# Two transformer blocks on one core: another order of the seven products of a weight block, and other places for its weight quarters

## The chip, the cores and the metric

The kernel runs on one core of a Trainium2 chip. The metric is the device time of one execution in microseconds (us). Before the change it is 1966.29 us, the median of three runs (1965.46 to 1967.71).

## The reference, cut to what matters

The reference computes two transformer blocks on a sequence of 512 tokens with 1024 channels, in float32. Each ends with a gated feed-forward part; the hidden width is 2816. The change touches only its first half, in both blocks:

```
h = rmsnorm(x, g)                      # [512, 1024]
a, u = h @ Wa, h @ Wu                  # each [1024, 2816]
hidden = silu(a) * u                   # [512, 2816]
x = x + hidden @ Wdown                 # not touched
```

In the first block Wa and Wu are the two halves of `w_ffn_in`, in the second they are `w_ffn_gate_2` and `w_ffn_up_2`.

## The kernel before, in words

TensorE (PE) gets float32 precision from three products of rounded halves: every operand is split into a high half (`wh`, a cast on ACT) and a low half (`wl`, a subtraction on VectorE, DVE), and one product is high x high + high x low + low x high (lines 1029 to 1031). Splitting a 128x1024 weight tile is therefore one cast on ACT (L170) and one subtraction on DVE (L171).

The hidden columns come in eleven slices of 256 columns of Wa and the same of Wu. The first two slices (`N_PLAIN`) are plain products (`gemm_quarters`, lines 275 to 277). Each of the other nine is a `Block`: a product of 2 x 2 quarters by Strassen's scheme in Winograd's form, seven products in place of eight. The rows of the weights are cut in two halves and the columns in two, which here are the slice of Wa and that of Wu. A product is 24 matmuls of 128x256 (2 column tiles, 4 steps of k, 3 halves), so a stage of nine blocks has 63 products or 1512 matmuls. Nine blocks in each of the two feed-forward parts: call them stage 1 and stage 2, and count blocks from 0.

The seven weight operands of a block are T1 to T7. T1, T2 and T3 are plain quarters of the weights. T5 and T7 are sums of two quarters that the DMA makes: SP loads one quarter into a tile, and then GpSimd's queue (POOL) issues a second transfer that adds the other quarter into it (`accum_op`, L994). T6 = T1 + T7 overwrites T1 (DVE, L1005), and T4 = T2 + T6 overwrites T2 (DVE, L1008). All activations' operands S1 to S7 are ready before the first block.

`woven` sets the order of the products: in a block 1, 2, then 3 of the block before, 6, 7, then 4 of the block before, 5. `play` goes through that list and splits two products ahead: while product n runs, `prep` of product n+2 is issued. `prep` takes a place for `wh` and one for `wl`, of which there are three each, so the cast of a product can start when the product three places earlier has been read. `prep` then makes the sums of T6 and T4, and last it issues a load of the block after: `prep` of 6 loads its T1, of 7 its T7, of 5 its T5, of 3 its T3, and of 1 its T2.

The places of the tiles: `raw` has three, which T1 (later T6), T5 and T7 share with all plain weight loads; T2 and T3 take places of `S`, of which there are 18, 16 of them with the activations' halves. A load waits until its place is free. The SP and POOL queues, like the engines, work in the order in which their instructions stand; a scheduler lays them out, near the order of the source. When a product is done, `after` copies or adds the sums in PSUM (ACT L1038, DVE L1040, L1043, L1048), and `out` makes the gated product (ACT L1129, DVE L1130, L1135). PSUM bank A holds the sums of products 1, 6, 5, 3, bank B product 2, bank C products 7 and 4.

Of the kernel before, what the change touches and what calls it, by code (L numbers as in the profile page):

```python
# [9 lines left out]
F32 = mybir.dt.float32  # L10
# [57 lines left out]
SLOTS = {"p": 32, "t": 12, "k": 3, "raw": 3, "wh": 3, "wl": 3}  # L68

MIX = {"q": 36}  # L70
FFN = {"S": 18}

STEP = 0.65
SB_FILL = (1.14, 1.5, 0.46)
# [5 lines left out]
N_PLAIN = 2  # L80
# [40 lines left out]
def run(gen):  # L121
    for _ in gen:
        pass


def build(tc, A, dump=None):
    nc = tc.nc
    with ExitStack() as es:
# [25 lines left out]
        def wtile(tag, shape, dt):  # L154
            if tag in SLOTS:
                return P.tile(shape, dt, tag=tag, name=tag, bufs=SLOTS[tag])
            return region["pool"].tile(shape, dt, tag=tag, name=tag, bufs=region["slots"][tag])
# [29 lines left out]
        def weights(w, k0, kn, c0, ncol):  # L187
            if low_engine["e"] is None:

                raw = wtile("raw", [128, kn, ncol], F32)  # L190
                nc.sync.dma_start(raw, w[k0 * 128:(k0 + kn) * 128, c0:c0 + ncol].rearrange("(k p) n -> p k n", p=128))
                wh = wtile("wh", [128, kn, ncol], F32R)
                wl = wtile("wl", [128, kn, ncol], F32R)
                nc.scalar.copy(wh, raw)
                nc.scalar.activation(wl, f(wh), AF.Copy, scale=-1.0)
                nc.gpsimd.dma_start(wl, raw, accum_op=ALU.add)
                return wh, wl
            raw = wtile("raw", [128, kn, ncol], F32)
            nc.sync.dma_start(raw, w[k0 * 128:(k0 + kn) * 128, c0:c0 + ncol].rearrange("(k p) n -> p k n", p=128))
            wh = wtile("wh", [128, kn, ncol], F32R)  # L200
            wl = wtile("wl", [128, kn, ncol], F32R)
            nc.scalar.copy(wh, raw)  # L202
            low_engine["e"].tensor_tensor(out=wl, in0=raw, in1=f(wh), op=ALU.subtract)  # L203
            return wh, wl
# [58 lines left out]
        def gemm_quarters(w, c0, X, evac, n0=0):  # L263

            ws = [weights(w, b, 4, c0, 256) for b in (0, 4)]
            for hf in range(2):
                ps = psum("gz"[hf])
                for n in range(2):
                    s = slice(n * 128, n * 128 + 128)
                    for k in range(KD):  # L270
                        wh, wl = ws[k // 4]
                        xh, xl = X.at(k, hf)
                        o = ps[:, n * 256:n * 256 + 256]
                        st, sp = n == 0 and k == 0, n == 1 and k == KD - 1
                        nc.tensor.matmul(o, wh[:, k % 4, s], xh, start=st, stop=False, skip_group_check=True)
                        nc.tensor.matmul(o, wh[:, k % 4, s], xl, start=False, stop=False, skip_group_check=True)
                        nc.tensor.matmul(o, wl[:, k % 4, s], xh, start=False, stop=sp, skip_group_check=True)
                for n in range(2):
                    evac(n0 + n, hf, ps[:, n * 256:n * 256 + 256])
# [62 lines left out]
        cols = small("cols", NVEC)  # L342
# [156 lines left out]
        for k in range(KD):  # L499
# [7 lines left out]
            for n, off in enumerate((0, 128, 512, 640, 256, 384)):  # L507
                s = slice(off, off + 128)
# [228 lines left out]
        for h in range(4):  # L737
# [20 lines left out]
            for c in range(2):  # L758
                run(gemm(w_in, KD, 7168 + 512 * h + 256 * c, H, ev_g, n0=2 * c))
                if c == 0:  # L760
                    ada_next()
                    for j in range(4):
# [6 lines left out]
                        s = new("t")  # L769
# [6 lines left out]
            for e in range(4):  # L776
# [10 lines left out]
                s = new("t")  # L787
# [46 lines left out]
        show("merged", [merged[n] for n in range(8)])  # L834
        lay_out(FFN)

# [76 lines left out]
        class Normed:  # L913
# [3 lines left out]
            def __init__(self):  # L917
                self.X = [new("p") for _ in range(KD)]
                self.Q = {}
                self.S = {}  # L920
# [51 lines left out]
        class Block:  # L972

            def __init__(self, rows, cols, X, out):
                self.rows, self.cols, self.X, self.out = rows, cols, X, out
                self.kn = len(rows[0])
                self.T, self.w, self.ps, self.sb = {}, {}, {}, {}
                self.done = set()  # L980
# [5 lines left out]

            def load(self, n):

                (i, j), more, tag = {1: ((1, 1), None, "raw"), 2: ((2, 1), None, "S"), 3: ((2, 2), None, "S"),
                                     5: ((1, 2), (1, 1), "raw"), 7: ((1, 2), (2, 2), "raw")}[n]  # L990
                t = self.T[n] = wtile(tag, [128, self.kn, 256], F32)
                nc.sync.dma_start(t, self.part(i, j))
                if more:
                    nc.gpsimd.dma_start(t, self.part(*more), accum_op=ALU.add)  # L994

            def prep(self, i):

                T = self.T
                wh = wtile("wh", [128, self.kn, 256], F32R)
                wl = wtile("wl", [128, self.kn, 256], F32R)  # L1000
                split(T[i], wh, wl)
                self.w[i] = wh, wl
                if i == 1:
                    T[6] = T.pop(1)
                    nc.vector.tensor_add(T[6], T[6], T[7])  # L1005
                if i == 2:
                    T[4] = T.pop(2)
                    nc.vector.tensor_add(T[4], T[4], T[6])  # L1008
                if i == 6:
                    del T[6]  # L1010

            BANK = {1: "A", 6: "A", 5: "A", 3: "A", 2: "B", 7: "C", 4: "C"}
# [38 lines left out]
        def play(blocks):  # L1051

            steps = woven(blocks)
            after = dict(zip(blocks, blocks[1:]))
            for i in (1, 7, 2, 5, 3):
                blocks[0].load(i)

            def prep(b, i):
                b.prep(i)
                load = {6: 1, 7: 7, 5: 5, 3: 3, 1: 2}.get(i)  # L1060
                if b in after and load:
                    after[b].load(load)
            for b, i in steps[:2]:
                prep(b, i)
            for n, (b, i) in enumerate(steps):
                if n + 2 < len(steps):
                    prep(*steps[n + 2])
                b.product(i)

        def woven(blocks):  # L1070

            steps = []
            for n, b in enumerate(blocks + [None]):
                a = blocks[n - 1] if n else None
                steps += [(c, i) for c, i in ((b, 1), (b, 2), (a, 3), (b, 6), (b, 7), (a, 4), (b, 5)) if c is not None]
            return steps

        class Split:
# [21 lines left out]
        def ffn_hidden(wa, ca, wu, cu, X):  # L1100

            hid = [new("p") for _ in range(2 * N_PLAIN)]
            sums = X.sums()
            act = {}

            def ev_a(n, hf, ps):
                s = new("t")[:, 0:256]
                if n not in act:
                    act[n] = new("t")
                nc.scalar.activation(s, ps, AF.Sigmoid)  # L1110
                nc.vector.tensor_mul(act[n][:, HS[hf]], ps, s)

            def ev_u(n, hf, ps):
                nc.vector.tensor_mul(hid[n][:, HS[hf]], ps, act[n][:, HS[hf]])
            for c in range(N_PLAIN):
                gemm_quarters(wa, ca + 256 * c, X, ev_a, n0=2 * c)
                gemm_quarters(wu, cu + 256 * c, X, ev_u, n0=2 * c)
                for _ in range(4):
                    next(sums, None)
            run(sums)  # L1120
            blocks = []
            for s in range(N_PLAIN, 11):
                hold = {}
                hid += [new("p") for _ in range(2)]

                def out(i, j, c, s=s, hold=hold):
                    if j == 1:
                        g = new("t")
                        nc.scalar.activation(g, c, AF.Sigmoid)  # L1129
                        nc.vector.tensor_mul(c, c, g)  # L1130
                    hold[i, j] = c
                    if (i, 1) in hold and (i, 2) in hold:
                        for e in range(2):
                            es = slice(e * 256, e * 256 + 256)
                            nc.vector.scalar_tensor_tensor(out=hid[2 * s + e][:, HS[i - 1]], in0=hold[i, 2][:, es], scalar=-1.0,  # L1135
                                                           in1=hold[i, 1][:, es], op0=ALU.mult, op1=ALU.mult)
                blocks.append(Block((range(0, 4), range(4, 8)), ((wa, ca + 256 * s), (wu, cu + 256 * s)), X, out))
            play(blocks)
            lay_out(MIX)
            return Split(hid, ["q" if 2 <= i < 20 else "p" for i in range(KF)])  # L1140
# [32 lines left out]
        w2 = A["w_in_2"]  # L1173
# [13 lines left out]
        for k0 in (0, 4):  # L1187
            raw = wtile("raw", [128, 4, 56], F32)
# [343 lines left out]
        for h in range(0, 8, 2):  # L1532
            t = new("k" if h < 4 else "q").rearrange("p (h c) -> p h c", h=2)
# [45 lines left out]
        bg.drain()  # L1579
        lay_out(FFN)  # L1580
        show("cat", [cat[n] for n in range(8)])
# [22 lines left out]
        for b in range(2):  # L1604
# [23 lines left out]
            for t in range(4):  # L1628
                for h in held:
                    products(t, *h)  # L1630
                s = new("t")
# [46 lines left out]
```

## Time and profile before

| | |
|---|---|
| median of three runs | 1966.29 us |
| the profiled execution | 1966.17 us |
| its span | 1964.5 us |
| stage 1, first matmul to last | 916.5 to 1124.5 us of the span |
| stage 2, first matmul to last | 1625.4 to 1832.7 us |
| TensorE busy over the span | 94% |
| DVE, ACT, POOL busy | 62%, 43%, 17% |

The span runs from the first to the last instruction on the core; the execution's own time is 1.7 us longer. TensorE's time counts as busy while any matmul is in its pipe, and a matmul stays there longer (0.28 us) than the distance to the next (0.12 us), so a short wait shows as less idle time than it costs.

### The profile page before, as it was taken

Reading aid. Unit: us, or ns where it says so; the run is one execution under the profiler, and the core shown is the slowest. Engines: PE = TensorE matmul, PEld = TensorE weight load, DVE = VectorE, ACT = ScalarE, POOL = GpSimd, SP = SyncE. Lnnn points to the kernel's source line nnn. Section 1 sums busy time; section 2 is a strip of 40 time slices with the busy share of each in tenths; the row PEclk is TensorE's granted clock in tenths of the full one; section 3 lists DMA queues with packets and bytes.
Section 4 is the critical chain, followed back from the end, with each engine's and each line's share of the span. In section 5 each row is a group of like instructions: output and inputs, shape, how many; then the busy total and the mean of one; then the engine's idle time right before and its main releaser. Section 6 shows DMA issues by size and latency. Waiting matters only on the chain. (4 is left out here: it accounts for less than half of the span.)

```text
span 1964.5 us, 28367 instructions
## 1 busy us (share of the span) xinstructions
PE 1847.1 (94%) x11145; PEld 1622.2 (83%) x11145; DVE 1211.6 (62%) x1980; ACT 844.9 (43%) x1400; POOL 334.1 (17%) x397
## 2 busy tenths in 40 slices
PE   6889999999999999999888899979999899889998
PEld 4678887888888898889888888858887799889887
DVE  7888875645465654656666642467577575666622
ACT  3556653233323223344444442474365544444522
POOL 3232221112020302011111002122234201111000
PEclk8999999999999999999999999979999999999999
DMA  7512222533334244426766523266453137666222
GB/s 230 187 54 67 64 74 92 164 113 110 124 107 135 78 148 151 160 65 164 158 150 151 134 93 116 71 161 152 96 143 104 44 97 155 156 155 168 95 88 75
DMA packets 224929, 238.29 MB, mean 121 GB/s; under 512 B 10902, under 2 KB 207524, under 8 KB 224796
## 3 DMA queue, kind: packets, MB, share of 16 engines
q1 hardware_dynamic: 199424, 197.91, 32.6%
q0 software_dynamic: 25024, 38.44, 10.7%
q8 instruction: 87, 1.43, 0.3%
q14 instruction: 46, 0.38, 0.1%
q10 hardware_dynamic: 348, 0.13, 0.0%
HBM read 217.56 MB, written 9.99 MB: 116 GB/s over the span
## 5 line engine op out<-in xcount | busy, mean ns | idle before, releaser
L203 DVE TENSOR_TENSOR wl<-raw,wh 128x1024 fp32r<-128x1024 f32 x190 | 236.8, 1246 | 223.7 <-ACT wh L202 222.2
L202 ACT CAST wh<-raw 128x1024 fp32r<-128x1024 f32 x190 | 197.9, 1041 | 387.2 <-PE ps_g L181 190.1
L180 PE MATMUL ps_g<-p,wh 128*128 128x512 f32 (+1 forms) x824 | 327.6, 402 | 8.4 <-DVE q L1184 3.7
L181 PE MATMUL ps_g<-p,wh 128*128 128x512 f32 (+1 forms) x824 | 325.7, 396 | 4.8 <-DVE p L455 2.8
L182 PE MATMUL ps_g<-p,wl 128*128 128x512 f32 (+1 forms) x824 | 324.8, 395 | 0.0
L180 PEld LDWEIGHTS ps_g<-p,wh 128*128 128x128 f32 x824 | 156.5, 191 | 46.2 <-issue 8.3
L181 PEld LDWEIGHTS ps_g<-p,wh 128*128 128x128 f32 x824 | 157.5, 191 | 36.5 <-DVE p L455 3.5
L182 PEld LDWEIGHTS ps_g<-p,wl 128*128 128x128 f32 x824 | 157.4, 191 | 34.7
L1031 PE MATMUL ps_g<-S,wl 128*128 128x256 f32 x576 | 164.4, 285 | 13.1 <-DVE wl L171 13.1
L1029 PE MATMUL ps_g<-S,wh 128*128 128x256 f32 x576 | 163.5, 284 | 1.5 <-ACT t L1038 1.5
L1030 PE MATMUL ps_g<-S,wh 128*128 128x256 f32 x576 | 163.1, 283 | 0.0
L233 PE MATMUL ps_g<-wh,p 128*128 128x256 f32 x512 | 145.8, 285 | 2.0 <-ACT wh L202 1.5
L234 PE MATMUL ps_g<-wl,p 128*128 128x256 f32 x512 | 143.3, 280 | 1.2 <-DVE wl L203 1.2
L235 PE MATMUL ps_g<-wh,p 128*128 128x256 f32 x512 | 143.2, 280 | 0.0
L1031 PEld LDWEIGHTS ps_g<-S,wl 128*128 128x128 f32 x576 | 110.6, 192 | 15.7 <-DVE wl L171 15.7
L171 DVE TENSOR_TENSOR wl<-raw,wh 128x1024 fp32r<-128x1024 f32 (+1 forms) x76 | 88.8, 1170 | 51.7 <-ACT wh L170 51.6
L180 PE MATMUL ps_g<-q,wh 128*128 128x512 f32 (+1 forms) x304 | 118.0, 388 | 1.5 <-DVE p L1510 1.5
L182 PE MATMUL ps_g<-q,wl 128*128 128x512 f32 (+1 forms) x304 | 117.1, 385 | 0.0
L181 PE MATMUL ps_g<-q,wh 128*128 128x512 f32 (+1 forms) x304 | 117.1, 385 | 0.0
L1029 PEld LDWEIGHTS ps_g<-S,wh 128*128 128x128 f32 x576 | 110.8, 192 | 1.9 <-ACT t L1038 1.9
L1030 PEld LDWEIGHTS ps_g<-S,wh 128*128 128x128 f32 x576 | 110.8, 192 | 0.0
L170 ACT CAST wh<-raw 128x1024 fp32r<-128x1024 f32 (+1 forms) x76 | 76.3, 1007 | 76.7 <-PE ps_g L1030 35.5
(435 smaller groups left out, 4421.0 us busy)
## 6 DMA issues: line engine op xcount, KB each, us to landing
raw<-in_w_in SPq DMA_DIRECT2D x108, 512.0 KB, 4.0
raw<-in_w_ffn_in SPq DMA_DIRECT2D x35, 512.0 KB, 4.7
raw<-in_w_ada SPq DMA_DIRECT2D x32, 512.0 KB, 3.5
raw<-in_w_ffn_up SPq DMA_DIRECT2D x22, 512.0 KB, 4.6
raw<-in_w_ffn_down SPq DMA_DIRECT2D x22, 512.0 KB, 3.2
wl<-raw POOLq DMA_DIRECT2D x20, 512.0 KB, 5.3
raw<-in_w_ffn_out SPq DMA_DIRECT2D x19, 512.0 KB, 3.5
S<-in_w_ffn_in SPq DMA_DIRECT2D x18, 512.0 KB, 4.3
```

Source lines behind the costliest of these rows:

```text
L171: nc.vector.tensor_sub(lo, src, f(hi))
L180: nc.tensor.matmul(ps, lh, rh, start=start, stop=False)
L181: nc.tensor.matmul(ps, lh, rl, start=False, stop=False)
L182: nc.tensor.matmul(ps, ll, rh, start=False, stop=stop)
L202: nc.scalar.copy(wh, raw)
L203: low_engine["e"].tensor_tensor(out=wl, in0=raw, in1=f(wh), op=ALU.subtract)
L233: nc.tensor.matmul(o, xh[:, ts], wh[:, i], start=k == 0 and t % 2 == 0, stop=False)
L234: nc.tensor.matmul(o, xh[:, ts], wl[:, i], start=False, stop=False)
L235: nc.tensor.matmul(o, xl[:, ts], wh[:, i], start=False, stop=k == KD - 1 and t % 2 == 1)
L1029: nc.tensor.matmul(o, wh[:, k, s], sh[:, k], start=st, stop=False, skip_group_check=True)
L1030: nc.tensor.matmul(o, wh[:, k, s], sl[:, k], start=False, stop=False, skip_group_check=True)
L1031: nc.tensor.matmul(o, wl[:, k, s], sh[:, k], start=False, stop=sp, skip_group_check=True)
```

## The change

The order of the products in a block becomes 1, 7, 3 of the block before, 6, 2, 4 of the block before, 5: products 2 and 7 change places. T6 = T1 + T7 is now made in the `prep` of 7 instead of that of 1.

T1, T2 and T3 no longer lie in `raw` and `S`. They take turns in four places w0 to w3: tile n of block b lies in place (3b + n - 1) modulo 4. `raw` with its three places is left to T5 and T7, and `S` shrinks from 18 places to 14.

The loads move: `prep` of 7 loads T5 of the next block, of 3 loads T1 of the next but one (3 belongs to the block before, hence distance 2), of 2 loads T2 of the next, of 4 loads T3 of the block that now runs, and of 5 loads T7 of the next but one. T1, T2, T3 of block 0 and T1 of block 1 are loaded after the first of the two plain slices; T7 and T5 of block 0 and T7 of block 1 when the plain slices are done.

```diff
-FFN = {"S": 18}
+FFN = {"S": 14, "w0": 1, "w1": 1, "w2": 1, "w3": 1}
...
-                (i, j), more, tag = {1: ((1, 1), None, "raw"), 2: ((2, 1), None, "S"), 3: ((2, 2), None, "S"),
-                                     5: ((1, 2), (1, 1), "raw"), 7: ((1, 2), (2, 2), "raw")}[n]
-                t = self.T[n] = wtile(tag, [128, self.kn, 256], F32)
+                (i, j), more = {1: ((1, 1), None), 2: ((2, 1), None), 3: ((2, 2), None),
+                                5: ((1, 2), (1, 1)), 7: ((1, 2), (2, 2))}[n]
+                t = self.T[n] = wtile("raw" if more else "w%d" % ((3 * self.b + n - 1) % 4), [128, self.kn, 256], F32)
                 nc.sync.dma_start(t, self.part(i, j))
                 if more:
                     nc.gpsimd.dma_start(t, self.part(*more), accum_op=ALU.add)
...
-                if i == 1:
+                if i == 7:
                     T[6] = T.pop(1)
                     nc.vector.tensor_add(T[6], T[6], T[7])
...
-            after = dict(zip(blocks, blocks[1:]))
-            for i in (1, 7, 2, 5, 3):
-                blocks[0].load(i)
+            for b, i in ((0, 7), (0, 5), (1, 7)):
+                blocks[b].load(i)
 
             def prep(b, i):
                 b.prep(i)
-                load = {6: 1, 7: 7, 5: 5, 3: 3, 1: 2}.get(i)
-                if b in after and load:
-                    after[b].load(load)
+                d, n = {7: (1, 5), 2: (1, 2), 5: (2, 7), 3: (2, 1), 4: (1, 3)}.get(i, (len(blocks), 0))
+                if b.b + d < len(blocks):
+                    blocks[b.b + d].load(n)
...
-                steps += [(c, i) for c, i in ((b, 1), (b, 2), (a, 3), (b, 6), (b, 7), (a, 4), (b, 5)) if c is not None]
+                steps += [(c, i) for c, i in ((b, 1), (b, 7), (a, 3), (b, 6), (b, 2), (a, 4), (b, 5)) if c is not None]
...
+            for c in range(N_PLAIN):
+                if c == 1:
+                    for b, i in ((0, 1), (0, 2), (0, 3), (1, 1)):
+                        blocks[b].load(i)
+                gemm_quarters(wa, ca + 256 * c, X, ev_a, n0=2 * c)
```

DVE, before, over the start of one block in the middle of stage 1. In its rows raw_9808 is T1 and then T6, raw_9843 is T7, S_9707 is T2 and then T4, and S_9775 is T3 of the block before; L171 is a subtraction of a split.

```order
L171 TENSOR_TENSOR wl_9935<-raw_9808,wh_9934 128x1024
L1005 TENSOR_TENSOR raw_9808<-raw_9808,raw_9843 128x1024
L1048 TENSOR_TENSOR t_9668<-ps_r_9677,t_9668 128x512
L171 TENSOR_TENSOR wl_9972<-S_9707,wh_9971 128x1024
L1130 TENSOR_TENSOR t_9668<-t_9668,t_9966 128x512
L1008 TENSOR_TENSOR S_9707<-S_9707,raw_9808 128x1024
L1135 SCALAR_TENSOR_TENSOR p_8643<-t_9768,t_9668 128x256
L1135 SCALAR_TENSOR_TENSOR p_8644<-t_9768,t_9668 128x256
L1043 TENSOR_TENSOR t_10000<-ps_r_9909,t_10000 128x512
L171 TENSOR_TENSOR wl_10004<-S_9775,wh_10003 128x1024
L171 TENSOR_TENSOR wl_10037<-raw_9808,wh_10036 128x1024
```

DVE, after, over the same stretch of another block of stage 1. Here w1_9082 is T1 and then T6 of block 3, raw_8977 its T7, w2_9145 its T2 and then T4, and w0_9177 is T3 of block 2.

```order
L1005 TENSOR_TENSOR w1_9082<-w1_9082,raw_8977 128x1024
L1047 TENSOR_TENSOR t_8971<-ps_r_8883,t_8971 128x512
L171 TENSOR_TENSOR wl_9276<-raw_8977,wh_9275 128x1024
L1122 TENSOR_TENSOR t_8971<-t_8971,t_9270 128x512
L1127 SCALAR_TENSOR_TENSOR p_8109<-t_9075,t_8971 128x256
L1127 SCALAR_TENSOR_TENSOR p_8110<-t_9075,t_8971 128x256
L171 TENSOR_TENSOR wl_9311<-w0_9177,wh_9310 128x1024
L1042 TENSOR_TENSOR t_9307<-ps_r_9115,t_9307 128x512
L171 TENSOR_TENSOR wl_9344<-w1_9082,wh_9343 128x1024
L171 TENSOR_TENSOR wl_9373<-w2_9145,wh_9372 128x1024
L1008 TENSOR_TENSOR w2_9145<-w2_9145,w1_9082 128x1024
```

The subtraction of T2 and the sum of T4 have moved from right behind the sum of T6 to the end of the stretch, behind the subtractions of T7, T3 and T6. The instructions and their number are the same (lines below the change count one less).

The SP queue, before, over the loads of one block (raw_9576 is T1 of a block, raw_9611 its T7, raw_9674 its T5):

```order
L992 DMA S_9543<-in_w_ffn_in 128x4x256
L992 DMA raw_9576<-in_w_ffn_in 128x4x256
L992 DMA raw_9611<-in_w_ffn_in 128x4x256
L992 DMA S_9707<-in_w_ffn_in 128x4x256
L992 DMA raw_9674<-in_w_ffn_in 128x4x256
```

The SP queue, after (raw_8977 and raw_9048 are T7 and T5 of block 3, w1_9082 and w2_9145 its T1 and T2, w0_9177 is T3 of block 2, raw_9209 is T7 of block 4):

```order
L992 DMA raw_8977<-in_w_ffn_in 128x4x256
L992 DMA raw_9048<-in_w_ffn_in 128x4x256
L992 DMA w1_9082<-in_w_ffn_in 128x4x256
L992 DMA w2_9145<-in_w_ffn_in 128x4x256
L992 DMA w0_9177<-in_w_ffn_in 128x4x256
L992 DMA raw_9209<-in_w_ffn_in 128x4x256
```

A block still has five loads on SP and two adding transfers on POOL; T7 of a block now stands first among its five, where T1 stood ahead of it before, and a whole block lies between it and the block that uses it.

## Rows read from the trace of the kernel before

**Rows 1.** The page: span, and busy time of each engine.
```profile
span 1964.5 us, 28367 instructions
PE 1847.1 (94%) x11145; PEld 1622.2 (83%) x11145; DVE 1211.6 (62%) x1980; ACT 844.9 (43%) x1400; POOL 334.1 (17%) x397
```

**Rows 2.** Line L1029: duration (min/median/max ns), first and last start; stage 1, then 2.
```profile
L1029 PE MATMUL ps_g<-S,wh x288: 277/283/386, 916.5 to 1121.3; 128*128 128x256 f32 x144
L1029 PE MATMUL ps_r<-S,wh x144: 283/283/284, 925.1 to 1124.1; 128*128 128x256 f32 x144
...
L1029 PE MATMUL ps_g<-S,wh x288: 277/283/415, 1625.4 to 1829.4; 128*128 128x256 f32 x144
L1029 PE MATMUL ps_r<-S,wh x144: 283/283/284, 1634.1 to 1832.3; 128*128 128x256 f32 x144
```

**Rows 3.** Waits of PE: us in total, times, longest; stage 1, then 2.
```profile
PE ps_z L1031 <- DVE wl L171: 13.9, 8, 2.2
PE ps_g L1031 <- DVE wl L171: 7.0, 7, 1.0
...
PE ps_g L1029 <- ACT t L1038: 1.5, 1, 1.5
...
PE ps_z L1031 <- DVE wl L171: 11.4, 8, 2.8
PE ps_g L1031 <- DVE wl L171: 6.0, 6, 1.0
```

**Rows 4.** Timeline of PE at one wait: start, duration, instruction, idle before.
```profile
955.75 0.28 PE L1029 MATMUL ps_z<-S,wh 128*128 128x256 f32 x1
955.87 0.28 PE L1030 MATMUL ps_z<-S,wh 128*128 128x256 f32 x1
958.09 0.39 PE L1031 MATMUL ps_z<-S,wl 128*128 128x256 f32 x1 [1.95 <-DVE wl L171]
```

**Rows 5.** Timeline of DVE at the start of the next block.
```profile
971.89 1.22 DVE L171 TENSOR_TENSOR wl<-raw,wh 128x1024 fp32r<-128x1024 f32 x1 [1.61 <-ACT wh L170]
978.30 1.23 DVE L1005 TENSOR_TENSOR raw<-raw 128x1024 f32<-128x1024 f32 x1 [5.18 <-DMA raw<-in_w_ffn_in]
979.45 0.68 DVE L1048 TENSOR_TENSOR t<-ps_r,t 128x512 f32<-128x512 f32 x1
980.05 1.21 DVE L171 TENSOR_TENSOR wl<-S,wh 128x1024 fp32r<-128x1024 f32 x1
...
981.78 1.22 DVE L1008 TENSOR_TENSOR S<-S,raw 128x1024 f32<-128x1024 f32 x1
982.92 0.75 DVE L1135 SCALAR_TENSOR_TENSOR p<-t 128x256 f32<-128x256 f32 x2
```

**Rows 6.** Timelines of SP and POOL: T7 of that block, its load and its adding transfer.
```profile
965.08 0.37 SPq L992 DMA_DIRECT2D raw<-in_w_ffn_in  x1
...
970.50 1.28 POOL L994 DMA_DIRECT2D raw<-in_w_ffn_in  x1 [16.32 <-DVE wl L171]
```

**Rows 7.** Windows in stage 2: busy us, granted clock, DMA share, GB/s.
```profile
1646.00:1650.00 4.00, 4.00 (x23) 4.00 (x23) 3.62 (x5) 1.00 (x1) 0.00 (x0) 0.60 0.37 102
1693.00:1697.00 4.00, 4.00 (x23) 4.00 (x22) 4.00 (x7) 2.26 (x4) 0.00 (x0) 0.58 0.00 0
```

**Rows 8.** DMA from 930 to 1090 us: queues, then issues with us to landing.
```profile
q1 hardware_dynamic: 18172, 18.05, 36.9%
q0 software_dynamic: 7295, 7.24, 30.8%
...
raw<-in_w_ffn_in SPq DMA_DIRECT2D x21, 512.0 KB, 4.8
raw<-in_w_ffn_in POOLq DMA_DIRECT2D x14, 512.0 KB, 7.5
```

**Rows 9.** Timeline of ACT before and at the start of stage 1.
```profile
899.71 0.70 ACT L170 CAST S<-p 128x256 fp32r<-128x256 f32 x2
...
915.19 1.05 ACT L170 CAST wh<-S 128x1024 fp32r<-128x1024 f32 x1 [7.02 <-PE ps_z L276]
```

More of the change, by code (lines that the diff above doesn't have):

```diff
@@ L972, in build, with __init__ @@
         class Block:
-            def __init__(self, rows, cols, X, out):
-                self.rows, self.cols, self.X, self.out = rows, cols, X, out
+            def __init__(self, b, rows, cols, X, out):
+                self.b, self.rows, self.cols, self.X, self.out = b, rows, cols, X, out
                 self.kn = len(rows[0])
@@ L1008, in prep @@
                     nc.vector.tensor_add(T[4], T[4], T[6])
-                if i == 6:
                     del T[6]
@@ L1114, in ev_u @@
                 nc.vector.tensor_mul(hid[n][:, HS[hf]], ps, act[n][:, HS[hf]])
[L1115 to L1120, printed above, removed]
             blocks = []
@@ L1136, in out @@
                                                            in1=hold[i, 1][:, es], op0=ALU.mult, op1=ALU.mult)
-                blocks.append(Block((range(0, 4), range(4, 8)), ((wa, ca + 256 * s), (wu, cu + 256 * s)), X, out))
+                blocks.append(Block(len(blocks), (range(0, 4), range(4, 8)), ((wa, ca + 256 * s), (wu, cu + 256 * s)), X, out))
+            for c in range(N_PLAIN):
[3 more added lines that the diff above has]
+                gemm_quarters(wa, ca + 256 * c, X, ev_a, n0=2 * c)
+                gemm_quarters(wu, cu + 256 * c, X, ev_u, n0=2 * c)
+                for _ in range(4):
+                    next(sums, None)
+            run(sums)
             play(blocks)
```

## The prediction

> **What bounds the kernel now.** First the page: TensorE is busy for 94% of a span of 1964.5 us and DVE, the next engine, for 1211.6 us [rows 1]. So TensorE sets the time, and what a change can win is TensorE's pauses; the question is which of them lie where the change is.
>
> Second, the starts of the matmuls of the two stages [rows 2]. Stage 1 runs from 916.5 to 1124.5 us, which is 208.0 us, and stage 2 from 1625.4 to 1832.7, which is 207.3. Two matmuls that wait for nothing start 0.12 us apart (955.75 and 955.87 in [rows 4]), so 1512 of them need 1512 x 0.12 = 181.4 us; a product of 24 takes 2.88 us and a block of seven 20.16. The stages lose 26.6 and 25.9 us, 52.5 together.
>
> Third, what TensorE waited for [rows 3]. Nearly all of it is a low half `wl` that DVE had not finished: 13.9 us in eight waits in bank B (product 2 of each block but the first) and 7.0 us in seven waits in bank A (product 6); in stage 2 it is 11.4 and 6.0 us. One other wait, 1.5 us for a sum in ACT's L1038, stands at the end of the stage.
>
> Fourth, why `wl` is late: DVE around the start of a block [rows 5]. The sum T6 = T1 + T7 starts at 978.30 after 5.18 us in which DVE stands still, and what it waited for is a DMA. The subtraction for product 2 stands behind it and starts only at 980.05. DVE works in order, so product 2 waits for a tile that it doesn't use: T7.
>
> Fifth, why T7 is late: the queues [rows 6]. SP issued its load at 965.08, POOL its adding transfer at 970.50, and the sum could start at 978.30. From issue to use that is 13.2 us. The load was given out in `prep` of 7 of the block before, three preps, or 3 x 2.88 = 8.6 us of TensorE's work, ahead of the `prep` that needs it. The missing 4.6 us come back in every block as DVE's standstill.
>
> **What the change is worth, part by part.** *The wait for T7.* The load of T7 is now issued in `prep` of 5 of two blocks earlier and used in `prep` of 7. Laying the new order out by hand from the durations of [rows 5, 9] (cast 1.05, subtraction or sum of 128x1024 1.22, sum from PSUM 0.68, gated pair 2 x 0.75 at most), with time 0 at product 1 of a block and the cast of a product starting when the product three earlier ends, the load is issued at about 13.8 and the sum wants it at 17.2 of the next block: 20.16 + 17.2 - 13.8 = 23.5 us for a path of 13.2. T5 has more than that. DVE's standstill should go in every block.
>
> *What is late next on DVE.* In the same layout DVE has per block seven subtractions and two sums of 1.22 (11.0 us), five to six steps from PSUM of 0.68 and the gated pair: about 16 us of 20.16. The subtractions end at 5.1 (product 6), 8.0 (2), 11.1 (4 of the block before), 13.8 (5), 16.6 (next 1), 20.1 (next 7), 22.6 (next 3). Their products begin at 8.64, 11.52, 14.40, 17.28, 20.16, 23.04 and 25.92. The smallest distance is 2.9 us, so TensorE waits for none. The wait of product 6 goes with that of product 2: it came because DVE, after the standstill, had its whole backlog to work off, and there is now none. Should it not go, it costs what the rows show (below).
>
> *The sum.* Each stage loses its time in three parts. The waits: 13.9 + 7.0 + 11.4 + 6.0 = 38.3 us in 29 waits. A wait costs TensorE more than the idle time: in [rows 4] the start comes 2.22 us after the last, of which 0.12 is normal and 1.95 is shown, and the matmul then takes 0.39 in place of 0.28, so 0.15 + 0.11 = 0.26 us more; 29 x 0.26 = 7.5 us. The clock: in two stretches of 4 us in stage 2, each right behind one of these waits, the granted clock is 0.60 and 0.58 [rows 7]. At full and half level that is 3.2 to 3.4 us at half speed in each, which lose half of that, 1.6 + 1.7 = 3.3 us. Together 49.1 us. From the other side: 52.5 less the wait at the end of each stage, which the change doesn't touch (about 1.65 each), is 49.2. The two agree.
>
> *What is moved at no cost, and its cover.* T3 has the shortest lead now: it is issued at about 11.2 (after `prep` of 4) and cast at 20.05, 9 us later, and only beyond some 12 us would TensorE stand. Plain loads land in 3.8 to 4.8 us in the median [rows 8]. T1 has 12 us, T2 17. Bounds: nothing if they land as now; if each landed 3 us later than TensorE can bear, 9 x 3 us a stage. I take nothing, the row being that of the same transfer. On SP a load that waits for its place holds up all behind it, but in the new order the places come free in the order in which the loads stand, so the lead above is that of the queue, too. The early loads into w0 to w3 wait for nothing that ends late: the places are new. POOL's adding transfers are as many as before, and each now waits less.
>
> *The start of a stage.* Product 7 is now second. Before it ACT still has the four last casts of activations, 0.35 us each (0.70 for two), which end some 1.4 us after the 915.19 of [rows 9]: the cast of T7 then runs from 916.6 to 917.6, its subtraction to 918.9, and product 7 asks for it at 916.5 + 2.88 + 0.24 = 919.6. It holds by 0.7 us. Bounds: 0 to 1 us a stage; I take 0.5 each, 1 us together.
>
> *The bottom line.* 49.2 - 1.0 = 48.2 us. The profiled execution took 1966.2 (its span and 1.7 us around it), 0.1 under the median, so no correction is due: 1966.2 - 48.2 = 1918.0 us. If the wait at the end of each stage went too, it would be 1918.0 - 3.3 - 1.0 = 1913.7, and if the start of each stage cost its full 1 us and three short waits of 1.26 us stayed in all, 1918.0 + 1.0 + 3.8, about 1923: 1913 to 1923 is this case's own range.
>
> **Rivals.** *DVE stays late at product 6.* The order moves T2's subtraction and the sum of T4 between products 6 and 4, so DVE's work comes in a row from 17 to 23 of each block. My layout gives it 2.9 us of air, but it takes each cast to start as soon as its place is free. If ACT's other steps (the sums L1038, the sigmoid) hold a cast up, the short waits of [rows 3], 7 + 6 of 1.0 us, stay: 13 x 1.26 = 16.4 us, and 1918 + 16 = 1934. For it speaks that DVE's work is the same in amount; against it, that today's backlog begins with a standstill of 5.18 us [rows 5] that has its own cause. 0.17.
>
> *The wait moves from T7 to T3: no gain.* SP's loads come in another order, and T3 is now loaded in the block that uses it. If it landed in 15 us in place of 4, TensorE would stand 3 us in each of 18 blocks, 54 us, more or less what is won: 1966. For it speaks its lead, the shortest of all; against it the landing times of [rows 8], about half of the lead at most. 0.05.
>
> *The transfers become the bound: slower.* In stage 1, from 930 to 1090 us, plain loads take 36.9% of 16 engines for 18.05 MB and adding ones 30.8% for 7.24 MB [rows 8]. A transfer of 512 KB (0.524 MB) so takes 0.369 x 160 x 0.524 / 18.05 = 1.71 us of all engines, an adding one 3.57. A block's five and two need 5 x 1.71 + 2 x 3.57 = 15.7 us. Over 23 us a block that was 68%, and over 20.16 it will be 78%. If the transfers cost more as they come closer together, the stage follows them: from 20.16 / 15.7 = 1.28 times today's price on they set the pace, and from 23.1 / 15.7 = 1.47 times on the kernel is slower than before. At 24 us a block it would be 18 x 0.9 = 16 us over today's time, about 1982. For it speaks that an adding transfer lands in 7.5 us, twice its 3.57; against it, that today's block has stretches in which nothing moves and others in which loads and adding transfers go side by side. 0.05. The Trainium skill (DMA: Bandwidth & Descriptors, section "Issuing engines are not separate DMA queues") says that transfers issued by SP and by GpSimd run on the same 16 engines and interleave. By that rule the earlier loads of T1 to T3 can stretch the adding transfer of T7, which speaks against this change, and the 7.5 us of [rows 8] agree with it; the sum above stays as it is, since T7's lead of 23.5 us bears a path 10 us longer.
>
> That the change doesn't reach its aim, with the sum of T6 still ahead of a subtraction that is due at once, can be left out: in the new order of DVE the next subtraction behind the sum is that of T7, the tile that the sum needs anyway, and the subtraction of T2 stands behind three others.
>
> **How the numbers follow.** The forecast, 1918.0, has 0.73; product 6 late, 1934, 0.17; T3 late, 1966, 0.05; transfers, 1982, 0.05. The range from 1913 to 1936 takes in the first two with their own spread and leaves out a little over 1 in 10. A measurement of this kernel can tell 0.2% (3.9 us) from no change: faster 0.90, within it 0.05, slower 0.05.
>
> **What would show it.** Right: DVE's L1005 no longer has idle time ended by a DMA; TensorE's waits for `wl` of L171 are gone or a few tenths in all; the stages take 182 to 184 us; the two stretches with a granted clock near 0.6 are gone; T7's load is issued over 20 us ahead of its sum; the first product 7 of a stage starts with less than 1 us of wait. Wrong: waits for `wl` in bank A at product 6 (first rival), a cast of T3 that waits for a DMA (second), a DMA share near 100% and landings well over 7.5 us (third). A pause of more than a few us elsewhere, before the first product of a stage above all, would break the sum at a place that I costed at nothing.

## The result, and the profile after

The changed kernel takes 1917.35 us in the median of four runs (1915.66 to 1918.32), the kernel before beside it 1965.88 (1964.07 to 1967.71): a ratio of 0.9752, 95% interval 0.9735 to 0.9769, or 48.5 us less. The forecast was 1918.0. The profiled execution has a span of 1916.2 us in place of 1964.5 [rows 1]; TensorE is busy for 96% of it. The page:

```profile
span 1916.2 us, 28365 instructions
PE 1833.7 (96%) x11145; PEld 1616.0 (84%) x11145; DVE 1217.7 (64%) x1980; ACT 847.0 (44%) x1400; POOL 334.8 (17%) x397
```

The first of the three matmuls has moved by a line, to L1028. Their starts, stage 1 and then stage 2 (columns as in [rows 2]):

```profile
L1028 PE MATMUL ps_g<-S,wh x288: 283/283/385, 919.7 to 1099.7; 128*128 128x256 f32 x144
...
L1028 PE MATMUL ps_r<-S,wh x144: 283/283/283, 922.6 to 1102.6; 128*128 128x256 f32 x144
...
L1028 PE MATMUL ps_g<-S,wh x288: 278/283/386, 1601.2 to 1781.2; 128*128 128x256 f32 x144
...
L1028 PE MATMUL ps_r<-S,wh x144: 283/283/283, 1604.1 to 1784.1; 128*128 128x256 f32 x144
```

The last triple adds 0.35 us, so stage 1 runs from 919.7 to 1102.95 and stage 2 from 1601.2 to 1784.45: 183.3 us each, where the products are 181.4 of work. Before they took 208.0 and 207.3 [rows 2]. The stages gave 24.7 + 24.0 = 48.7 us. What else moved: stage 1 starts 3.2 us later than in the one profile of before, 500.9 us between the stages became 498.3, and the 131.8 us behind stage 2 stayed. 48.7 - 3.2 + 2.6 is 48.1 of the span's 48.3. The 3.2 us are no effect of the change that could be shown: they arise in the first 60 us, and the profiles of the other kernels of this study have stage 1 start anywhere from 917.8 to 920.9, the changed kernel itself in a second profile at 919.5. The one profile of before, at 916.5, is earlier than all of them, also than those of kernels that differ from it in the stages alone (e3_t7_first 919.2, e8_no_add 920.1).

What TensorE waited for from 900 to 1110 us (us in total, times, longest), answering to [rows 3]:

```profile
PE ps_g L181 <- DVE p L171: 2.0, 1, 2.0
PE ps_g L1028 <- ACT t L1037: 1.5, 1, 1.5
PE ps_g L180 <- ACT p L170: 0.6, 1, 0.6
```

Not one wait for `wl` is left; the first and the third row lie behind the stage's end. In stage 2 the view lists nothing at all. The 1.8 us that stage 2 takes beyond its products are other work, which TensorE does where it waits for L1037 in stage 1; before the change the same 14 small matmuls (there L1609) stood at that place, from 1825.09:

```profile
1776.89 1.72 PE L1610 MATMUL ps_g<-eye,p 128*128 128x128 f32 x14
```

DVE over the start of a block, answering to [rows 5]:

```profile
989.98 1.23 DVE L171 TENSOR_TENSOR wl<-w,wh 128x1024 fp32r<-128x1024 f32 x1 [0.27 <-ACT wh L170]
991.12 0.68 DVE L1122 TENSOR_TENSOR t<-t 128x512 f32<-128x512 f32 x1
991.73 1.22 DVE L1005 TENSOR_TENSOR w<-w,raw 128x1024 f32<-128x1024 f32 x1
992.86 0.68 DVE L1047 TENSOR_TENSOR t<-ps_r,t 128x512 f32<-128x512 f32 x1
993.46 1.22 DVE L171 TENSOR_TENSOR wl<-raw,wh 128x1024 fp32r<-128x1024 f32 x1
```

L1005 has no bracket: it waited for nothing. Its T7 was the first of the two loads that SP's queue shows from 968.19:

```profile
968.19 6.72 SPq L992 DMA_DIRECT2D raw<-in_w_ffn_in  x2
```

991.73 - 968.19 = 23.5 us from issue to use, where the path of [rows 6] took 13.2. The transfers and the clock over the middle of stage 1 (from:to, us, busy us of each engine, granted clock, DMA share, GB/s), first before, then after:

```profile
930.00:1090.00 160.00, 141.60 (x1154) 138.96 (x1154) 101.55 (x122) 67.44 (x82) 17.49 (x14) 1.00 0.68 159
```

```profile
930.00:1090.00 160.00, 160.00 (x1336) 160.00 (x1335) 119.31 (x141) 78.15 (x95) 17.97 (x14) 1.00 0.72 175
1610.00:1770.00 160.00, 160.00 (x1336) 160.00 (x1335) 118.98 (x140) 79.63 (x96) 17.99 (x14) 1.00 0.74 175
```

TensorE is busy for all of the 160 us, at a granted clock of 1.00 in stage 2, too, where [rows 7] had two stretches near 0.6. DVE works for about as long in all, and for more of each us. The DMA shares of these windows can't be compared as they stand: the changed kernel has issued the last of the stage's loads before 1090 us (the share is 0.36 from 1070 to 1080 and 0.17 from 1080 to 1090). Over five whole blocks, 935 to 1035.8 us, it is 0.77 at 184 GB/s.

### The profile page after: what moved, and what is told of

Its sections match the earlier page's. It is cut to its first block, busy times and chain, and to the rows that moved or that the text cites. A ratio compares the mean times of both kernels' runs of the same rounds, so it can differ in the third digit from the quotient of the medians.

```text
span 1916.2 us, 28365 instructions
## 1 busy us (share of the span) xinstructions
PE 1833.7 (96%) x11145; PEld 1616.0 (84%) x11145; DVE 1217.7 (64%) x1980; ACT 847.0 (44%) x1400; POOL 334.8 (17%) x397
## 5 line engine op out<-in xcount | busy, mean ns | idle before, releaser
L1028 PE MATMUL ps_g<-S,wh 128*128 128x256 f32 x576 | 163.2, 283 | 1.5 <-ACT t L1037 1.5
L1029 PE MATMUL ps_g<-S,wh 128*128 128x256 f32 x576 | 163.0, 283 | 0.0
L170 ACT CAST wh<-w 128x1024 fp32r<-128x1024 f32 x90 | 94.3, 1048 | 111.5 <-PE ps_g L1029 65.9
L171 DVE TENSOR_TENSOR wl<-w,wh 128x1024 fp32r<-128x1024 f32 x90 | 110.0, 1222 | 52.2 <-ACT wh L170 52.1
L1028 PEld LDWEIGHTS ps_g<-S,wh 128*128 128x128 f32 x576 | 110.6, 192 | 1.9 <-ACT t L1037 1.9
L1029 PEld LDWEIGHTS ps_g<-S,wh 128*128 128x128 f32 x576 | 110.6, 192 | 0.0
```

The lines of the kernel that those rows point to most:

```text
L171: nc.vector.tensor_sub(lo, src, f(hi))
L1028: nc.tensor.matmul(o, wh[:, k, s], sh[:, k], start=st, stop=False, skip_group_check=True)
L1029: nc.tensor.matmul(o, wh[:, k, s], sl[:, k], start=False, stop=False, skip_group_check=True)
```

## The experiments

Medians (of four runs; e7 and e9 of ten), ratios to the kernel before on the same chip, and the stages' lengths as above, from one profiled execution each:

| run | us | ratio (95%) | stage 1, 2 |
|---|---|---|---|
| a1_after (the change again) | 1917.65 | 0.9742 (0.9725 to 0.9759) | 183.3, 183.3 |
| e1_old_order | 1915.79 | 0.9734 (0.9717 to 0.9751) | 183.3, 183.3 |
| e2_old_loads | 1917.40 | 0.9746 (0.9727 to 0.9765) | 183.3, 184.1 |
| e9_late_t7 | 1959.93 | 0.9982 (0.9966 to 0.9997) | 201.9, 201.1 |
| e8_no_add | 1919.72 | 0.9764 (0.9742 to 0.9787) | 183.3, 183.3 |
| e3_t7_first | 1945.66 | 0.9886 (0.9866 to 0.9906) | 205.4, 189.8 |
| e4_sum_behind | 1929.05 | 0.9804 (0.9788 to 0.9820) | 188.6, 187.9 |
| e6_add_t2 | 1919.13 | 0.9757 (0.9737 to 0.9777) | 183.3, 183.2 |
| e7_add_t12 | 1968.82 | 1.0007 (0.9989 to 1.0026) | 209.1, 210.2 |
| e11_add_t2_t7 | 1935.71 | 0.9864 (0.9837 to 0.9890) | 188.7, 191.2 |
| e5_tail | 1920.37 | 0.9761 (0.9744 to 0.9779) | 183.2, 183.2 |
| e10_tail | 1916.33 | 0.9760 (0.9737 to 0.9783) | 181.5, 181.5 |

The repeat was expected so: 

> The changed kernel again, for comparison with the runs beside it on the same chip: 1915 to 1919 us.

**The loads without the order.** e1_old_order is the changed kernel with the old order:

```diff
-(b, 1), (b, 7), (a, 3), (b, 6), (b, 2), (a, 4), (b, 5)
+(b, 1), (b, 2), (a, 3), (b, 6), (b, 7), (a, 4), (b, 5)
...
-                if i == 7:
+                if i == 1:
                     T[6] = T.pop(1)
...
-{7: (1, 5), 2: (1, 2), 5: (2, 7), ...
+{7: (1, 5), 6: (1, 2), 5: (2, 7), ...
```

> The changed kernel's four places and its loads, with the old order of the products (1, 2, 3 of the block before, 6, 7, 4 of the block before, 5) and the sum of T6 again in prep of 1, so that DVE's instructions stand as before the change: the sum of T6 right ahead of the subtraction of product 2. Theory (the wait for T7 alone cost the time, and a load a block earlier takes it away): DVE's work of about 16 us fits in 20.16, no standstill at L1005, 1915 to 1921 us. Rival (the order of the products is needed, because the subtraction of product 2 still stands behind the sum and DVE's backlog at product 6 remains): 1934 us or more, with TensorE waiting for wl in bank B or A in each block.

Measured: 1915.79, the whole gain, and no wait for `wl`. DVE's instructions stand as before the change, and its waits from 930 to 1090 us hold no line on L1005. So the subtraction of product 2 may stand right behind the sum of T6, if T7 is there.

**The order without the loads.** e2_old_loads is the kernel before, with this:

```diff
-(b, 1), (b, 2), (a, 3), (b, 6), (b, 7), (a, 4), (b, 5)
+(b, 1), (b, 7), (a, 3), (b, 6), (b, 2), (a, 4), (b, 5)
...
-                if i == 1:
+                if i == 7:
                     T[6] = T.pop(1)
...
-                load = {6: 1, 7: 7, 5: 5, 3: 3, 1: 2}.get(i)
+                load = {7: 7, 2: 1, 5: 5, 3: 3, 1: 2}.get(i)
```

> The new order of the products with the old places: raw with three places for T1, T5 and T7, and T2 and T3 in S. T7 takes the place of the T6 of the block before, which is free after the sum of T4, at about 9.2 of a block; T1 is loaded behind it. Theory: the path of 13.2 us ends at 22.4, the sum wants T7 at 17.2, DVE stands 5.2 us, and the subtraction of product 7 behind it ends at about 25.4 where TensorE wants it at 23.3: 2.1 us a block and 0.26 of restart, 16 x 2.4 = 38 us and some more at product 3, 1955 to 1970 us. Rival (the order alone brings the gain, since the subtraction of T2 no longer stands behind the sum): 1916 to 1930 us.

Measured: 1917.40, the whole gain again, and the expectation was wrong. SP's queue and DVE of this run show why:

```profile
1003.22 0.37 SPq L992 DMA_DIRECT2D raw<-in_w_ffn_in  x1
...
1007.69 7.97 SPq L992 DMA_DIRECT2D raw<-in_w_ffn_in  x2
...
1014.05 1.22 DVE L171 TENSOR_TENSOR wl<-raw,wh 128x1024 fp32r<-128x1024 f32 x1
...
1031.67 1.22 DVE L1005 TENSOR_TENSOR raw<-raw 128x1024 f32<-128x1024 f32 x1
```

The second of the two loads ends with the pair at 1015.66, so it was issued at 1015.29, right behind the subtraction of product 7 (1014.05 to 1015.27): T7 took the place of the T7 before it and not, as the expectation had it, that of T6 (which T1 takes, at 1003.22). From there to the sum at 1031.67 are 16.4 us. In the old order the same place is given back at 8.0 of a block and wanted at 16.6, 8.6 us; in the new order the last use of a T7 (its subtraction) stands right behind its first (the sum of T6), and the place is free for all the rest of the block. The new order is itself a longer lead. Whether it is the lead was asked next, with T1 in the place of T7 and T7 in that of T6:

```diff
-                load = {7: 7, 2: 1, 5: 5, 3: 3, 1: 2}.get(i)
+                load = {7: 1, 2: 7, 5: 5, 3: 3, 1: 2}.get(i)
```

> As e2_old_loads (the new order of the products, the old places), but T1 of the next block takes the place of T7 and T7 that of T6, which is free only at about 9.2 of a block (after the sum of T4) in place of 2.9 before its start. All else is as in e2_old_loads. Theory (e2_old_loads was as fast as the changed kernel because T7 there takes its own old place, at once free after its subtraction, and so has 17 us of lead): with 8 us of lead for a path of 11.5 to 13.2 us the subtraction of product 7 ends at 23.7 to 25.4 of the block where TensorE wants it at 23.3, so 0.4 to 2.1 us and 0.26 in 16 blocks, 11 to 38 us more: 1928 to 1957 us, with DVE standing still at L1005 for a DMA. Rival (the order of the products alone makes the gain, whatever the lead): 1916 to 1920 us.

Measured: 1959.93, nearly all the gain lost, by a change of two numbers in the loads under the new order. TensorE's and DVE's waits in stage 1:

```profile
PE ps_r L1028 <- DVE t L1047: 6.2, 7, 1.7
PE ps_r L1030 <- DVE wl L171: 4.7, 8, 0.8
...
DVE raw L1005 <- DMA raw<-in_w_ffn_in: 31.4, 7, 5.5
```

The standstill is back, 4.5 us a block. The loss, 18.6 + 17.8 = 36.4 us by the stages, stands at the upper end of what was expected, and the median 3 us above it; the profiled execution, at 1954.42, was the fastest of the ten. Two things were not in the expectation: a second instruction is caught behind the sum, L1047, which reads bank C and so frees it for product 7 (6.2 us of waits in stage 1), and the granted clock is 0.91 in two windows of 20 us (995 to 1015 and 1035 to 1055), worth 1.8 us each. What slowed the other nine further isn't shown. The load of T1 moved as well, but no wait of TensorE in the stage stands at product 1. It isn't the order of the products, then, but what it does to T7's lead.

**The path of T7 alone.** e8_no_add is the kernel before, with `if more:` ahead of the adding transfer made `if n == 5:`.

> The kernel before, without the adding transfer on T7 (T7 is then one quarter in place of a sum of two, which changes what is computed); order, places and all loads stay. T7's path falls from 13.2 us to the landing of a plain load, about 5 us, against a lead of 8.6. Theory: no standstill at L1005, product 2 and product 6 no longer wait although the subtraction of product 2 still stands behind the sum: 1916 to 1924 us. Rival (DVE's order is what is too tight, and the landing only adds to it): waits of about 1 us at product 6 remain, 1930 us or more.

Measured: 1919.72; no wait for `wl`, none of L1005, in the old order with the old places and loads. The short waits at product 6 are gone as well: they were the echo of the standstill. What is left of DVE's order costs nothing. The edit also takes one of a block's seven transfers away, and the adding ones that are left land in 6.1 us in place of 7.5, so e8 by itself doesn't part the path from the traffic; e2 and e9, which move the same transfers and differ in the lead, do.

**Half a cure.** e3_t7_first exchanges two loads of the kernel before:

```diff
-                load = {6: 1, 7: 7, 5: 5, 3: 3, 1: 2}.get(i)
+                load = {6: 7, 7: 1, 5: 5, 3: 3, 1: 2}.get(i)
```

> The kernel before with one exchange: prep of 6 loads T7 of the next block and prep of 7 loads its T1, so that T7 is issued first, at about 5.1 of a block in place of 8.0. Theory (lead against path, with the slack between): the standstill of DVE falls from 4.6 to about 1.7 us, the subtraction of product 2 ends at 21.3 where TensorE wants it at 23.3, and the short waits at product 6 go with it: 1916 to 1924 us from a two-number edit. Rival (each us of lead is worth a us of the standstill, and no more): the issue is only 1.7 to 2.9 us earlier, 16 blocks x 1.7 to 2.9 is 27 to 46 us less, 1920 to 1939 us, with waits at product 6 still there.

Measured: 1945.66, which neither expected: stage 1 gained 2.6 us, stage 2 17.5. Of the eight sums of stage 1 all had a standstill, 39.8 us together; in stage 2 they were 23.0 us, five of them 1.7 to 2.4. One of each:

```profile
981.06 1.22 DVE L1005 TENSOR_TENSOR raw<-raw 128x1024 f32<-128x1024 f32 x1 [5.51 <-DMA raw<-in_w_ffn_in]
...
1720.54 1.23 DVE L1005 TENSOR_TENSOR raw<-raw 128x1024 f32<-128x1024 f32 x1 [1.76 <-DMA raw<-in_w_ffn_up]
```

The sum of stage 2 has the 1.7 us that were worked out. In stage 1 T7 was issued at 965.77, its adding transfer at 971.48, and it was there at 981.06, after 15.3 us; in stage 2 at 1708.60, 1713.69 and 1720.54, after 11.9. The subtraction of product 2 had 2.0 us to spare by the expectation (21.3 against 23.3); with so little the path's own spread decides. Why the adding transfer took 9.6 us in one stage and 6.9 in the other stays open.

**The place in DVE's order alone.** e4_sum_behind is the kernel before, with T6's sum behind the subtraction of product 2:

```diff
-                if i == 1:
+                if i == 2:
                     T[6] = T.pop(1)
+                    nc.vector.scalar_tensor_tensor(out=T[6][:, 0, 0:1], in0=wl[:, 0, 0:1], scalar=0.0, ...
                     nc.vector.tensor_add(T[6], T[6], T[7])
-                if i == 2:
...
```

> The kernel before, its order of products, places and loads, with the sum of T6 held back on DVE behind the subtraction of product 2 by a one-column instruction that adds zero times that wl to T1 (16 instructions more a stage pair, about 0.1 us each). T7's path stays 13.2 us. Theory (it is the place in the order of DVE that hurts, not the late landing): the subtraction of product 2 is done at 19.5 of the block, the sum runs at about 21.4 when T7 has landed, the subtractions of products 3 and 6 end at 25.5 and 26.6 where TensorE wants them at 26.2 and 29.0: 1916 to 1924 us. Rival (T7 has to come earlier; what stands behind its sum doesn't matter): 1960 to 1968 us, the waits only move to products 3 and 6.

Measured: 1929.05. Four fifths of the gain (2.0% of 2.5) come without an earlier load; the rest is in part the wait moved on to product 3 (three waits for `wl` in each stage, 2.3 and 3.3 us) and what follows it. T7's path is unchanged, so it is the place behind a waiting instruction that cost most. Stage 1 is 5.3 us over 183.3, 3.5 of it at one place, where the T7 of block 1 came late. DVE and TensorE there, and the window behind (columns as above):

```profile
938.97 1.23 DVE L1007 TENSOR_TENSOR raw<-raw 128x1024 f32<-128x1024 f32 x1 [3.88 <-DMA raw<-in_w_ffn_in]
...
943.24 0.42 PE L1032 MATMUL ps_g<-S,wl 128*128 128x256 f32 x1 [1.74 <-DVE wl L171]
```

```profile
943.00:947.00 4.00, 3.76 (x19) 3.76 (x19) 3.66 (x5) 0.63 (x1) 0.00 (x0) 0.57 0.56 171
```

**The transfers as a bound.** e6_add_t2 adds a quarter to T2, e7_add_t12 to T1 and T2, e11_add_t2_t7 to T2 and a second time to T7. The places stay; of the edits only the entries that add transfers are shown:

```diff
-2: ((2, 1), None), 3: ...
+2: ((2, 1), (1, 1)), 3: ...            # e6, e7, e11
+{1: ((1, 1), (2, 1)), ...              # e7
+for _ in range(2 if n == 7 else 1):    # e11, ahead of the adding transfer
```

> The changed kernel with one more adding transfer a block: T2 gets a second quarter added, which changes what is computed. Engine time of the transfers by today's price: 15.7 + 3.57 = 19.3 us a block of 20.16, 96%. T2 has 17 us of lead for a path of 13.2. Theory (the transfers are not the bound below 20.16 us a block): 1915 to 1921 us. Rival (transfers that come closer cost more, contention decides): 1930 us or more, waits for wl of T7 or T5.

> The changed kernel with two more adding transfers a block, on T1 and T2, which changes what is computed. By today's price 15.7 + 7.1 = 22.9 us of engine time a block: the transfers should set the pace at 22.9 in place of 20.16, 18 x 2.7 = 49 us more, about 1966 us, with a DMA share near 100% in the stages. Rival (an adding transfer's share counts time in which its packets wait for each other, and the engines have room): 1916 to 1930 us, with the share near 90% and no wait of TensorE.

> The changed kernel with two more adding transfers a block, one on T2 and a second one on T7, which changes what is computed. The transfers have the same engine time as in e7_add_t12 (22.9 us a block), but T7 and T2 have 23.5 and 17 us of lead where T1 had 12. If e7_add_t12 was slow because the 16 engines were full: about 1966 us again, with a DMA share over 0.9. If it was slow because T1's path with an adding transfer is longer than its lead: 1916 to 1930 us.

Measured: 1919.13, 1968.82, 1935.71. e6 kept TensorE free of waits for weights at a share of 0.96 from 935 to 1035 us, as the 19.3 us a block had it (0.90 over 930 to 1090, with the end of the stage's loads). The middle of stage 1 in e7 and in e11:

```profile
930.00:1090.00 160.00, 145.46 (x1136) 142.02 (x1135) 100.07 (x121) 65.45 (x82) 35.06 (x28) 0.96 0.94 200
```

```profile
930.00:1090.00 160.00, 156.03 (x1291) 154.89 (x1290) 114.74 (x136) 75.41 (x92) 36.70 (x29) 1.00 1.04 219
```

e7 met the forecast of 1966 and yet not by the reason given for it. e11 has as many transfers and moves them faster, 219 GB/s against 200, in (188.7 - 1.7) / 9 = 20.8 us a block where e7 took 23.0: the 16 engines were not full in e7. ACT there waited for T1's tile, whose path with an adding transfer is longer than its lead of 12 us. In one block T1's load went out at 1008.92 (the first of three), its adding transfer at 1013.90, and the cast could start at 1025.05, 16.1 us after the issue:

```profile
1008.92 8.00 SPq L992 DMA_DIRECT2D w<-in_w_ffn_in  x3
...
1013.90 1.39 POOL L994 DMA_DIRECT2D w<-in_w_ffn_in  x1
...
1025.05 1.05 ACT L170 CAST wh<-w 128x1024 fp32r<-128x1024 f32 x1 [6.60 <-DMA w<-in_w_ffn_in]
```

e11 lies above the 1916 to 1930 that were expected for this reason, and far from 1966: there it is again T6's sum that waits (20.1 us in 7 times, DVE's L1006 for a DMA), behind a T7 with two adding transfers. The share counts the packets' time in both queues and passes 1; it is no measure of how much room is left.

**The wait at the end of a stage.** e5_tail exchanges the last two products, e10_tail the two ahead of them:

```diff
+            steps[-2:] = steps[:-3:-1]                    # e5
+            steps[-4:-2] = steps[-3], steps[-4]           # e10
```

> The changed kernel, and in each stage the last two products exchanged: product 4 of the last block before its product 3. Product 3 adds to bank A, which ACT has to copy after product 5; with 4 between, ACT has 2.88 us for it. Theory: the wait of 1.5 us for ACT's L1037 goes, with its restart 1.7 us a stage, 3.4 us in all; and the last chain becomes shorter (a gated pair straight from PSUM in place of a sum, a sigmoid, a product and the pair), which may take up to 2 us from the wait for the hidden tile after each stage: 1910 to 1914 us. Rival (what follows the stage waits for the last hidden tile anyway, and the wait reappears there): no change, 1916 to 1918 us.

> The changed kernel, with product 4 of the block before and product 5 exchanged in the last block of each stage, so that the stage ends 6, 2, 5, 4 of the block before, 3, 4. Between product 5 and product 3, which both use bank A, there is now one product (2.88 us) in which ACT copies bank A. Theory: the wait of 1.5 us for ACT's L1037 and its restart go, 1.7 us a stage, 3.4 us in all: 1913 to 1915 us. Rival (the wait is given back at the start of what follows the stage): 1916 to 1918 us.

e5 measured 1920.37 and did not test its theory: the scheduler laid half of product 3 ahead of product 4, and the wait of 1.55 us stayed. e10 did what it says in stage 1: the wait for L1037 is gone, and both stages take 181.5 us, the products and nothing else. Yet its 1916.33 can't be told from the change. TensorE behind stage 1 (end 1101.94) and stage 2 of e10:

```profile
1103.76 0.50 PE L181 MATMUL ps_g<-p,wh 128*128 128x512 f32 x1 [1.16 <-DVE p L171]
...
1107.37 0.50 PE L181 MATMUL ps_g<-p,wh 128*128 128x512 f32 x1 [1.89 <-DVE p L171]
...
1780.86 2.84 PE L1611 MATMUL ps_g<-eye,p 128*128 128x128 f32 x24
1783.45 0.48 PE L1620 MATMUL ps_g<-wh,p 128*128 128x512 f32 x1
```

The same matmuls started at 1107.87 and 1785.48 in the changed kernel, 4.9 and 1.0 us behind its stages' ends; here it is 5.4 and 2.6. Of 1.8 us a stage 0.5 and 1.6 are given back at once. In stage 2 there was no wait to win: the 14 small matmuls that filled the place in the changed kernel now stand behind the stage with the other ten (x24 above), so the 1.6 us are work that moved. The forecasts of e5 and e10 had counted this stage as a wait, as the prediction had. Behind stage 1 the granted clock of e10 then fell, to 0.82 and 0.75 in the windows 1106 to 1110 and 1110 to 1114, worth 0.7 + 1.0 us, where the changed kernel has 1.00. No version of the study beats the change by more than the intervals.

## Why the prediction was right

- The bound, T6's sum waiting for T7 at the head of DVE: shown by e8_no_add, which shortens T7's path, and from the other side by e9_late_t7, which shortens its lead (against e2_old_loads, with the same transfers).
- The sum: 49.2 us less 1.0 for the starts of the stages. The stages gave 48.7. The 1.0 was not needed at all: the subtraction of T7 in block 0 ran from 920.80 to 922.0, where product 7 asks for it at 919.7 + 3.12 = 922.8. Of the 0.5 that are missing from 49.2, 0.3 lie at the ends of the stages, which keep 1.8 us each (183.3 against the 181.5 of e10_tail) where 1.65 was counted; the rest is rounding. The clock's two stretches went with the waits in front of them, as counted.
- A wrong reading in the check of that sum: it took the end of each stage for a wait. [rows 3] list one in stage 1 alone; in stage 2 the time is that of 14 other matmuls, 1.72 us, so the two ways of counting agree because that work is about as long as the wait. The 3.3 us that the lower end of the range takes off could not have come from waits at both ends.
- In part luck: that the total fell within 0.7 us of 1918.0. The prediction costed what lies outside the stages at nothing; there the profiles differ by 3.2 us one way and 2.6 the other, which nearly cancel.
- The leads: 23.5 us for T7, as worked out, and no wait of TensorE for T3 with its lead of 9. The last block of a stage, which the layout left aside, has less: no next block stands between, so T3's load goes out at 1086.45 and its cast begins at 1089.99, as soon as it has landed. Product 3 begins only at 1097.09, behind the wait for L1037, so that costs nothing.
- First rival (product 6 late): its waits end with the standstill in e1, e2 and e8, whatever DVE's order, but for one of 0.6 us in stage 2 of e2. Third rival (the transfers): the price per transfer held, and the share that it gives sets no pace. By [rows 8] 15.7 us a block or 78% were expected; the five whole blocks show 0.77, 15.5 us, and TensorE waits for nothing in them. e6 has 0.96 with no wait of TensorE either, and e11 reaches 1.04 at a higher rate than e7. The adding transfers land in 6.1 us, sooner than the 7.5 of [rows 8]. By the Trainium skill (DMA: Bandwidth & Descriptors, "Issuing engines are not separate DMA queues") transfers of both issuers share the engines and interleave; e6 agrees, with adding transfers that land in 8.0 us in place of 6.1 and no effect on the time, since the leads bear it.
- What the prediction didn't see: it put the gain down to the loads moved ahead, and gave the new order no share in it. Each of the two parts brings all of it alone, and together they bring it once.

## What to carry to other kernels

Where an in-order engine stands at an instruction that waits for a transfer, compare the lead (from the release of the tile's place to its first use) with the path, and look for what sets the release: an order in which a tile's last use follows closely on its first can lengthen the lead enough, as an earlier load does (here from 8.6 to 16.4 us, where the earlier load gave 23.5). Two parts of a change that feed the same wait don't add. A cure with two us to spare was decided here by the spread of the transfers (11.9 to 15.3 us for the same path). A window that runs past the last loads of a stage shows a lower DMA share than the stage has.

## What the runs showed beside that

The 2.6 us gained between the stages are in good part the clock: in the kernel before, the windows 1128 to 1132 and 1132 to 1136 us, behind stage 1, have a granted clock of 0.80 and 0.77, worth 0.8 + 0.9 us, and those at the same place after the change (1102 to 1114) 1.00. Where the other 0.9 us come from isn't shown. In e5_tail, where one wait of 2.13 us stands at that place in place of 0.6 and 2.0 with matmuls between, the window 1106 to 1110 is at 0.65. Which of two waits of like length is followed by a fall could not be told beforehand from these rows.
